# mLSTM values as one group of 512 columns in four PSUM banks, a value rank padded to 128 columns, and a bonus sum in another pair of banks

## The chip, the cores and the metric

The kernel runs on one core of a Trainium2 chip. The metric is the device time of that core in microseconds (us). The core has five engines that each run their own instructions in order: TensorE (PE, with its weight loads PEld), VectorE (DVE), ScalarE (ACT), GpSimd (POOL) and SyncE (SP), which issues most of the transfers.

## The reference

Two layers over 512 positions of 2048 features. Each layer normalises x, multiplies it by one wide matrix, cuts the product into the inputs of three branches, gates and joins their outputs, and multiplies by an output matrix:

```
for l in range(DEPTH):                       # 2 layers
    h = rms_norm(x, norm_g[l])               # 512 x 2048
    proj = h @ w_in[l]
    (ml_qk, ml_v, ml_i, ml_f, ml_o, ml_z, mla_cq, mla_ckv, mla_kr, mla_z,
     rw_mix, rw_z) = jnp.split(proj, offsets, axis=-1)     # ml_v: 512 columns
    y_ml  = mlstm_branch(...)                # 4 heads of 128
    y_mla = mla_branch(...)                  # 8 heads, softmax attention
    y_rw, v_first = rwkv7_branch(...)        # 8 heads of 64
    mixed = concat([silu(ml_z) * y_ml, silu(mla_z) * y_mla, silu(rw_z) * y_rw])
    x = x + mixed @ w_out[l]
return rms_norm(x, final_norm_g)

# in rwkv7_branch: in layer 1 the values are mixed with those of layer 0,
    v = v + (v_first - v) * jax.nn.sigmoid(v0 + (v @ v1) @ v2)     # v1: 512 x 32
# and the bonus is added to the output
    y = y + jnp.sum(r_h * k_h * r_k, axis=-1, keepdims=True) * v_h
```

Everything is float32. Sums over features run on TensorE.

## The kernel before

**Precision.** A float32 product is made of three passes over values split into a high and a low part: high times high, high times low, low times high (`passes`). ACT writes the high part of a weight block (L150), DVE or for some blocks POOL the low part (L151). Names follow: `raw_mv`, `whi_mv`, `wlo_mv` for the weights of the group mv; `xh`, `xl` for the normalised input, which lies feature-major in 16 blocks of 128 features.

**The projection as background work.** The wide matrix is cut into groups, named in `ORDER`: rk, rr, rv, rz for RWKV7, mq, mk, mv, mo, mz for the mLSTM, cq, ck, az for the attention, misc for narrow ones. A group has 256 columns of the matrix, as four weight blocks of 512 KB (`ws` streams them through two buffers in this order). `gemm` is a generator: for each block it issues 24 matmuls in two steps. All groups but mv give feature-major results: 512 positions are the moving columns, the weights are the stationary operand (L239). The mLSTM values must lie position-major, so for mv the input is stationary and the 256 weight columns move (`tmajor`, L235): 192 matmuls of 256 columns for each half of each 128-position block, two halves sharing a bank. The result goes through ACT (L597) to `mv_d` in DRAM.

**The foreground.** `rw_pair` runs four times a layer, for two RWKV7 heads each: a chain of small triangular solves by doublings. Its steps, in order, end in the PSUM tiles psw and psa (low-rank decays), psn (norm), psbo (bonus sum, `head_sum`, L714), psG, psTk, psTa, psTv (transposes), psQ, psR, psT, psX (doublings, L919), psW, psM, psN, psY. DVE and ACT work between two such steps, and background matmuls are to cover it: `bg.along` takes so many background steps for each step of the foreground. Then `rw_states` with `ml_head(0)` and `ml_head(1)`; then the attention's low-rank inputs with `ml_head(2)` and `ml_head(3)`; then `attention`.

**ml_head** makes scores (psSm), a weighted sum (psN), normalises it (`den`, `c`, `hn`, L1123 to L1141, with a square root on ACT), transposes it (psHT), gates it (`go`, L1151) and writes it to `mix_d` (L1152). Its SBUF pool is closed behind head 3, and the attention's pool `lp`, which holds the values `Vh` and `Vl`, takes its place: a write to `Vh` or `Vl` comes after the last reading of what lay there, the write of `go` to DRAM included.

**The attention** takes for each pair of heads the rotary part (psqr, then `rope` L1234 to L1237), queries and keys (psqn, pskn, L1263, split to qnh, qnl, knh, knl), values (psv, L1291, to Vh and Vl), scores (pssc), softmax (pp), transposes (pspt) and the weighted sum (pso).

**PSUM.** Eight banks: tag a (`bank`) two, tag b (`bank2`) two, tag g (`gbank`) three, tag h (`bank3`) one. Projection groups and psqr, psqn, pskn, psv take g; psbo, psSm, psHT take h; psG and ml_head's psN take b.

**Order.** Which instruction of an engine comes when is set at build time by a scheduler that simulates a timeline; on the chip each engine keeps that order.

Of the kernel before, what the change touches and what calls it, by code (L numbers as in the profile page):

```python
# [67 lines left out]
_REST = ["mq0", "mk0", "mv0", "mo0", "mz0", "rz1", "mq1", "mk1", "mv1", "mo1", "mz1", "cq0", "cq1", "ck0", "az0", "az1", "az2", "az3"]  # L68
# [5 lines left out]
def trunk(ctx, tc, a, out):  # L74
# [103 lines left out]
    def passes(hi, lo, xh, xl):  # L178
        return ((hi, xh), (hi, xl), (lo, xh))
# [38 lines left out]

    bg = Work()

    def gemm(l, name, finish, tmajor=False):

        def run():
            ps = [gbank(f"pg{u}_{name}{l}") for u in range(2)]
            xh, xl = xT[l]
            for kq in range(4):
                hi, lo = ws.get()
                for u in range(2):
                    for tb in range(2 * u, 2 * u + 2) if tmajor else (0,):
# [79 lines left out]
    def columns(l, name):  # L309
# [207 lines left out]
    for l in range(DEPTH):  # L517
# [72 lines left out]
        def park(kind, pr, l=l):  # L590

            def finish(u, ps):
                j = pr * 2 + u
                t = stage(f"{kind}{l}_{j}")
                if kind == "mv":
                    for b in range(2):
                        act(t[:, b * 256:b * 256 + 256], ps[:, b * 256:b * 256 + 256], AF.Copy,  # L597
                            scale=kept["rs"][:, 2 * u + b:2 * u + b + 1])
                    dma(mv_d[pr][:, u * 512:u * 512 + 512], t)
                    return  # L600
                if kind not in ("cq", "ck"):
                    ps = normed(stage(f"n{kind}{l}_{j}"), ps)
                if kind in ("mq", "mk"):
                    c = (0 if kind == "mq" else 4) + j
                    t, y = ps, t
                    act(y, ps, AF.Identity, scale=pc(R_CW + 24 + c), bias=pc(R_CB + c))
                    for d in range(1, 4):
                        stt(y[:, d:T], ps[:, 0:T - d], pc(R_CW + (3 - d) * 8 + c), y[:, d:T],
                            ALU.mult, ALU.add)
                    silu2(t, y, t)  # L610
                elif kind in SHIFT:
                    shift(t, ps, SHIFT[kind] + j)
                    if kind == "rv" and l > 0:
                        if j == 0:
                            kept["v1"] = bank(f"psv1_{l}")
                        mm(kept["v1"][0:32, :], lhsT=v1[:, j, :], rhs=t, start=(j == 0), stop=(j == 3))
                        if j == 3:
                            kept["vv"] = vv = rp.tile([128, T], F32R, name=f"vv{l}")
                            for r in (0, 64):
                                nc.scalar.copy(vv[r:r + 32], kept["v1"][0:32, :])  # L620
                                tt(vv[r + 32:r + 64], kept["v1"][0:32, :], vv[0:32].bitcast(F32), ALU.subtract)
                elif kind in ("az", "rz", "mz"):
                    silu2(t, ps, t)
                elif kind == "mo":
                    act(t, ps, AF.Tanh, scale=0.5)
                else:
                    normed(t, ps)
                dma(vf_d[j] if kind == "rv" and l == 0 else park_d[PARK[kind] + j], t)
            return finish

        for name in ORDER[l]:
            pr = int(name[2]) if name != "misc" else 0
            finish = misc_out if name == "misc" else park(name[0:2], pr)
            gemm(l, name, finish, tmajor=name[0:2] == "mv")
        if l == 0:
            x_tiles(0)
            for q in range(4):
# [43 lines left out]
            act(m[own], raw[own], AF.Copy)  # L681
            tt(m[other], raw[own], m[own].bitcast(F32), ALU.subtract)
        if l > 0:
            v1 = rp.tile([128, 4, 32], F32, name=f"v1_{l}")
            nc.gpsimd.dma_start(v1, a["rw_v1"][l - 1].rearrange("(k p) r -> p k r", p=128))
            raw = rp.tile([32, T], F32, tag="UV", name=f"v2r_{l}")
            nc.gpsimd.dma_start(raw, a["rw_v2"][l - 1])
            v2 = rp.tile([128, T], F32R, name=f"v2_{l}")
            for r in (0, 32):
                act(v2[r:r + 32], raw, AF.Copy)  # L690
                tt(v2[r + 64:r + 96], raw, v2[0:32].bitcast(F32), ALU.subtract)


        def rw_pair(p, l=l):
# [861 lines left out]
```

## Time and profile before

| | |
|---|---|
| median of 3 runs | 1966.4 us (1966.26 to 1967.19) |
| profiled execution | 1964.04 us, of which 1962.3 us from the first to the last instruction (the span) |
| granted TensorE clock, mean | 0.997 |
| busy share of the span | PE 98%, PEld 82%, DVE 63%, ACT 44%, POOL 7%, DMA engines 44% |
| matmuls of the projection with 256 columns (L235) | 768, 192 for each half group and layer |

A busy share is the time in which an engine had an instruction in work; PE's is nearly the whole span, since a matmul's record reaches from its start to the end of its drain and the next has started long before. So for TensorE the distance from start to start tells more than the durations. The rest of the span, some 30 us, is where PE has nothing in work.

### The profile page before, as it was taken

What the parts mean: (1) busy time and instruction counts of PE and PEld (TensorE: products, weight loads), DVE (VectorE), ACT (ScalarE), POOL (GpSimd) and SP (SyncE); (2) the same over time, 40 slices, a digit from 0 to 9 for tenths busy, and PEclk for the clock granted to TensorE, in tenths of its full rate; (3) what the DMA queues carried; (4) which work ended last, traced back from release to release, by engine and by line L of the source; (5) the groups of instructions that cost most, each with busy time, mean ns of one, the idle gap of its engine ahead of it and who ended that gap; (6) DMA issues with size and microseconds to landing.
All of it is one profiled execution on the core that took longest, in us unless ns stands there. A gap on an engine that the chain in (4) does not pass through costs nothing. (4 is left out here: it accounts for less than half of the span.)

```text
span 1962.3 us, 31796 instructions
## 1 busy us (share of the span) xinstructions
PE 1932.2 (98%) x12544; PEld 1607.1 (82%) x12544; DVE 1245.6 (63%) x2179; ACT 863.5 (44%) x1509; POOL 136.4 (7%) x168
## 2 busy tenths in 40 slices
PE   8999999999999999999999999999999999999998
PEld 6888888888888878788888788988878888788886
DVE  6876776685766398533366558676847676884343
ACT  6534352434556356422263234433434564563233
POOL 4010010100000031000001001010100000210000
PEclk9999999999999999999999999999999999999999
DMA  5443444335655443334444444344345564343334
GB/s 178 131 141 106 126 127 119 115 110 173 188 167 177 120 119 121 103 136 133 135 111 138 121 122 129 118 131 122 106 125 189 167 209 137 105 133 115 118 121 158
DMA packets 246394, 264.86 MB, mean 135 GB/s; under 512 B 49972, under 2 KB 178174, under 8 KB 246246
## 3 DMA queue, kind: packets, MB, share of 16 engines
q1 hardware_dynamic: 245398, 261.88, 43.8%
q8 instruction: 98, 1.61, 0.3%
q0 software_dynamic: 848, 0.97, 0.2%
q14 instruction: 50, 0.41, 0.1%
HBM read 212.45 MB, written 50.35 MB: 134 GB/s over the span
## 5 line engine op out<-in xcount | busy, mean ns | idle before, releaser
L1405 PE MATMUL po<-whi_o,mh 128*128 128x512 f32 x512 | 200.2, 391 | 0.1
L1405 PE MATMUL po<-whi_o,ml 128*128 128x512 f32 x512 | 199.3, 389 | 0.0
L151 DVE TENSOR_TENSOR wlo_o<-raw_o,whi_o 128x1024 fp32r<-128x1024 f32 x64 | 78.3, 1225 | 188.7 <-ACT whi_o L150 187.6
L1405 PE MATMUL po<-wlo_o,mh 128*128 128x512 f32 x512 | 187.8, 390 | 0.0
L150 ACT ACTIVATE whi_o<-raw_o 128x1024 fp32r<-128x1024 f32 x64 | 67.7, 1059 | 204.7 <-PE po L1405 168.2
L1405 PEld LDWEIGHTS po<-whi_o,mh 128*128 128x128 f32 x512 | 96.1, 188 | 20.1 <-DVE Vl L254 0.6
L1405 PEld LDWEIGHTS po<-wlo_o,mh 128*128 128x128 f32 x512 | 96.0, 188 | 20.0
L1405 PEld LDWEIGHTS po<-whi_o,ml 128*128 128x128 f32 x512 | 96.2, 188 | 19.7
L239 PE MATMUL pg_az<-xl,whi_az 128*128 128x512 f32 x256 | 100.7, 393 | 0.0
L239 PE MATMUL pg_az<-xh,whi_az 128*128 128x512 f32 x256 | 100.6, 393 | 0.0
L239 PE MATMUL pg_az<-xh,wlo_az 128*128 128x512 f32 x256 | 99.5, 394 | 0.0
L235 PE MATMUL pg_mv<-whi_mv,xh 128*128 128x256 f32 x256 | 72.9, 285 | 0.0
L235 PE MATMUL pg_mv<-whi_mv,xl 128*128 128x256 f32 x256 | 72.7, 285 | 0.0
L235 PE MATMUL pg_mv<-wlo_mv,xh 128*128 128x256 f32 x256 | 72.4, 285 | 0.0
L770 POOL TENSOR_TENSOR bk<-kk,Ei 64x512 f32<-64x512 f32 x16 | 26.5, 1657 | 505.2 <-DVE kk L757 176.5
L151 DVE TENSOR_TENSOR wlo_az<-raw_az,whi_az 128x1024 fp32r<-128x1024 f32 x32 | 39.1, 1223 | 31.0 <-ACT whi_az L150 30.8
L239 PEld LDWEIGHTS pg_az<-xh,wlo_az 128*128 128x128 f32 x256 | 48.1, 188 | 9.5
L239 PEld LDWEIGHTS pg_az<-xh,whi_az 128*128 128x128 f32 x256 | 48.1, 188 | 9.4
L239 PEld LDWEIGHTS pg_az<-xl,whi_az 128*128 128x128 f32 x256 | 48.2, 188 | 9.3
L239 PE MATMUL pg_rk<-xh,whi_rk 128*128 128x512 f32 x128 | 50.9, 401 | 1.3 <-ACT xh L252 1.3
L239 PE MATMUL pg_rk<-xl,whi_rk 128*128 128x512 f32 x128 | 51.5, 403 | 0.0
L150 ACT ACTIVATE whi_az<-raw_az 128x1024 fp32r<-128x1024 f32 x32 | 33.7, 1053 | 39.7 <-PE pg_az L239 26.6
(576 smaller groups left out, 5547.7 us busy)
## 6 DMA issues: line engine op xcount, KB each, us to landing
raw_o<-in_w_out_dram SPq DMA_DIRECT2D x64, 512.0 KB
raw_az<-in_w_in_dram SPq DMA_DIRECT2D x32, 512.0 KB
raw_rk<-in_w_in_dram SPq DMA_DIRECT2D x16, 512.0 KB
raw_rr<-in_w_in_dram SPq DMA_DIRECT2D x16, 512.0 KB
raw_rv<-in_w_in_dram SPq DMA_DIRECT2D x16, 512.0 KB
raw_rz<-in_w_in_dram SPq DMA_DIRECT2D x16, 512.0 KB
raw_mq<-in_w_in_dram SPq DMA_DIRECT2D x16, 512.0 KB
raw_mk<-in_w_in_dram SPq DMA_DIRECT2D x16, 512.0 KB
```

What stands on the lines that cost most here:

```text
L150: act(hi, raw, AF.Copy)
L151: (nc.gpsimd if name[0] == "u" or name in ("misc0_0", "misc0_1") else nc.vector).tensor_tensor(lo, raw, hi.bitcast(F32), ALU.subtract)
L235: mm(ps[u][:, (tb % 2) * 256:(tb % 2) * 256 + 256], lhsT=xx[:, sl], rhs=w[:, i, :], start=(k == 0 and n == 0 and tb % 2 == 0), stop=(k == ...
L239: mm(ps[u], lhsT=w[:, i, u * 128:(u + 1) * 128], rhs=xx, start=(k == 0 and n == 0), stop=(k == 15 and n == 2))
L770: nc.gpsimd.tensor_tensor(bk[q, :, slot, :], x[q].rearrange(c64, t=64), Ei[q].rearrange(c64, t=64), ALU.mult)
L1405: mm(pss[tb], lhsT=xx[:, sl], rhs=w, start=(k == korder[0] and j == 0), stop=(k == korder[15] and j == 2))
```

## The change

Three things. The mLSTM values become one group, `mv`, of all 512 columns, in the place of mv0; mv1 leaves the order, so that mo1 follows mk1. The generator `gemm_rows` issues it: eight weight blocks of 256 rows by 512 columns (the same 512 KB), for each block four banks (three of tag g and the one of tag h) of six matmuls of 512 columns, and a step behind every second bank: 16 steps, as many as mv0 and mv1 had together. That makes 192 matmuls of 512 columns a layer in place of 384 of 256. Four ACT copies of 512 columns and eight transfers of 256 columns replace eight copies of 256 columns and four transfers of 512. Second, `v1` is padded with zeros from 32 to 128 columns, and the matmul of L616 writes 128 rows. Third, psbo takes its bank from tag b, since tag h is now held by the group mv.

```diff
-_REST = ["mq0", "mk0", "mv0", "mo0", "mz0", "rz1", "mq1", "mk1", "mv1", "mo1", "mz1", "cq0", ...
+_REST = ["mq0", "mk0", "mv", "mo0", "mz0", "rz1", "mq1", "mk1", "mo1", "mz1", "cq0", ...
...
-    def gemm(l, name, finish, tmajor=False):
+    def gemm(l, name, finish):
...
-                    for tb in range(2 * u, 2 * u + 2) if tmajor else (0,):
-                        sl = slice(tb * 128, (tb + 1) * 128)
-                                if tmajor:
-                                    mm(ps[u][:, (tb % 2) * 256:(tb % 2) * 256 + 256], lhsT=xx[:, sl],
-                                       rhs=w[:, i, :], start=(k == 0 and n == 0 and tb % 2 == 0),
-                                       stop=(k == 15 and n == 2), skip_group_check=True)
...
+    def gemm_rows(l, name, finish):
+
+        def run():
+            ps = [(gbank, bank3, gbank, gbank)[tb](f"pg{tb}_{name}{l}") for tb in range(4)]
+            xh, xl = xT[l]
+            for kh in range(8):
+                hi, lo = ws.get()
+                for tb in range(4):
+                    sl = slice(tb * 128, (tb + 1) * 128)
+                    for i in range(2):
+                        k = kh * 2 + i
+                        for n, (w, xx) in enumerate(passes(hi, lo, xh[k], xl[k])):
+                            mm(ps[tb], lhsT=xx[:, sl], rhs=w[:, i, :], start=(k == 0 and n == 0),
+                               stop=(k == 15 and n == 2))
+                    if kh == 7:
+                        finish(tb, ps[tb])
+                        if tb == 3:
+                            bg.done.add(name)
+                    if tb % 2:
+                        yield
         bg.todo.append(run())
...
+            if name == "mv":
+                for kh in range(8):
+                    ws.add(mv_columns(l, kh), (2, 512), f"mv{l}_{kh}")
+                continue
...
-                if kind == "mv":
-                    for b in range(2):
-                        act(t[:, b * 256:b * 256 + 256], ps[:, b * 256:b * 256 + 256], AF.Copy,
-                            scale=kept["rs"][:, 2 * u + b:2 * u + b + 1])
-                    dma(mv_d[pr][:, u * 512:u * 512 + 512], t)
-                    return
...
-                        mm(kept["v1"][0:32, :], lhsT=v1[:, j, :], rhs=t, start=(j == 0), stop=(j == 3))
+                        mm(kept["v1"], lhsT=v1[:, j, :], rhs=t, start=(j == 0), stop=(j == 3))
...
+        def values_out(tb, ps, l=l):
+            t = stage(f"mv{l}_{tb}")
+            act(t, ps, AF.Copy, scale=kept["rs"][:, tb:tb + 1])
+            for pr in range(2):
+                dma(mv_d[pr][:, tb * 256:tb * 256 + 256], t[:, pr * 256:pr * 256 + 256])
...
-            v1 = rp.tile([128, 4, 32], F32, name=f"v1_{l}")
+            v1 = rp.tile([128, 4, 128], F32, name=f"v1_{l}")
+            nc.vector.memset(v1[:, :, 32:128], 0.0)
...
-            ps = head_sum(bo, "AR", "psbo", bank3)
+            ps = head_sum(bo, "AR", "psbo", bank2)
```

The change also moves other instructions, since the scheduler is run anew. Three places. A number behind a name tells the layer's head, pair or block apart; the last one is the tile's.

On PE in layer 0, pair 3, between the steps psR and psT of the first doubling, before (18 projection matmuls stand between the two, of which the first two and the last are shown; psT is eight instructions, of which two are shown):

```order
L825 MATMUL psR_3_3435<-UV_3_3332,GG_3_3150 64x64 x2
L235 MATMUL pg_mv_5063<-wlo_mv_0_4995,xh_0_132 128x256
L235 MATMUL pg_mv_5063<-whi_mv_0_4994,xh_1_133 128x256
...
L235 MATMUL pg_mv_5064<-whi_mv_0_4994,xl_2_150 128x256
L919 MATMUL psT_3_3493<-Qa_3_3398,X_3_3303 32x32 x4
L919 MATMUL psT_3_3492<-Qa_3_3398,X_3_3303 32x32 x4
```

The steps of the pair and the projection take turns there. In the changed kernel at the same place:

```order
L851 MATMUL psR_3_3413<-UV_3_3332,GG_3_3150 64x64 x2
L232 MATMUL pg_mk_4810<-xl_3_151,whi_mk_0_4734 128x512
L232 MATMUL pg_mk_4810<-xh_3_135,wlo_mk_0_4735 128x512
...
L232 MATMUL pg_mk_4811<-xh_1_133,wlo_mk_0_4735 128x512
L945 MATMUL psT_3_3459<-Qa_3_3376,X_3_3303 32x32 x4
L945 MATMUL psT_3_3458<-Qa_3_3376,X_3_3303 32x32 x4
```

Pair 3 of layer 0 now lies beside mk0, of which eight matmuls of 512 columns stand between the two steps; the group mv lies beside pair 2 in layer 0 and beside pairs 1 and 2 in layer 1.

On PE at the end of layer 1's head 3, where the attention begins, before (twelve psqn of the attention's first head and twelve psqr come only behind these rows):

```order
L239 MATMUL pg_az_15974<-xh_12_8412,wlo_az_3_16039 128x512
L239 MATMUL pg_az_15974<-xh_13_8413,whi_az_3_16038 128x512
L239 MATMUL pg_az_15974<-xl_13_8429,whi_az_3_16038 128x512
L1145 MATMUL psHT_3_15555<-idf,hn_3_15550 128x128
L239 MATMUL pg_az_15974<-xh_13_8413,wlo_az_3_16039 128x512
L1145 MATMUL psHT_3_15555<-idf,hn_3_15550 128x128 x3
L239 MATMUL pg_az_15974<-xh_14_8414,whi_az_3_16038 128x512
...
L239 MATMUL pg_az_15974<-xl_15_8431,whi_az_3_16038 128x512
L239 MATMUL pg_az_15974<-xh_15_8415,wlo_az_3_16039 128x512
L1263 MATMUL psqr_0_16116<-cqh_0_15182,whi_uqr_0_16069 128x512
```

There the transpose psHT stands among matmuls of az, and az outlasts it. In the changed kernel (the last chunk of psN, six pskn of head 1, twelve psqn of head 2, the transpose psHT, six pskn of head 2):

```order
L1140 MATMUL psN_3_1_15066<-mvh_3_15059,mel_3_15142 128x130
L1289 MATMUL pskn_1_15858<-ckh_0_14807,whi_uqk_1_15798 128x512
...
L1289 MATMUL pskn_1_15858<-ckh_1_14808,wlo_uqk_1_15799 128x512
L1289 MATMUL psqn_2_15978<-cqh_0_14799,whi_uqk_2_15837 128x512
...
L1289 MATMUL psqn_2_15978<-cqh_3_14802,wlo_uqk_2_15838 128x512
L1171 MATMUL psHT_3_15172<-idf,hn_3_15167 128x128 x4
L1289 MATMUL pskn_2_15995<-ckh_0_14807,whi_uqk_2_15837 128x512
...
L1289 MATMUL pskn_2_15995<-ckh_1_14808,wlo_uqk_2_15838 128x512
L1352 MATMUL pssc_0_2_15903<-knh_0_15791,qnh_0_15780 128x384
```

The projection az now ends before head 3 is done, and head 3's last steps stand among the attention's first ones: psv of the first pair, psqn and pskn of two heads come ahead of psHT.

On DVE at the same place, before:

```order
L1132 TENSOR_TENSOR c_3_15533<-c_3_15533,var_3_15532 128x4
L270 RECIPROCAL c_3_15533<-c_3_15533 128x4
L1134 SCALAR_TENSOR_TENSOR c_3_15533<-c_3_15533,den_3_15531 128x4
L1141 TENSOR_SCALAR hn_3_15550<-psN_3_0_15448,c_3_15533 128x128
L1141 TENSOR_SCALAR hn_3_15550<-psN_3_1_15449,c_3_15533 128x128
L1150 SCALAR_TENSOR_TENSOR go_3_15560<-go_3_15560,gz_3_15561 128x512
L542 TENSOR_TENSOR sg_naz_6_16086<-pg_az_15973,rb_9678 128x512
L254 TENSOR_TENSOR ml_12_17496<-mr_12_17493,mh_12_17495 128x512
L1151 SCALAR_TENSOR_TENSOR go_3_15560<-psHT_3_15555,prm_291,go_3_15560 128x512
```

There `hn` follows the normalisation at once. In the changed kernel:

```order
L1158 TENSOR_TENSOR c_3_15150<-c_3_15150,var_3_15149 128x4
L285 RECIPROCAL c_3_15150<-c_3_15150 128x4
L1160 SCALAR_TENSOR_TENSOR c_3_15150<-c_3_15150,den_3_15148 128x4
L269 TENSOR_TENSOR knl_1_15866<-pskn_1_15858,knh_1_15865 128x512
L1167 TENSOR_SCALAR hn_3_15167<-psN_3_0_15065,c_3_15150 128x128
L1167 TENSOR_SCALAR hn_3_15167<-psN_3_1_15066,c_3_15150 128x128
L1176 SCALAR_TENSOR_TENSOR go_3_15177<-go_3_15177,gz_3_15178 128x512
L1177 SCALAR_TENSOR_TENSOR go_3_15177<-psHT_3_15172,prm_291,go_3_15177 128x512
L269 TENSOR_TENSOR Vl_0_15803<-psv_0_0_15804,Vh_0_15802 128x512
L269 TENSOR_TENSOR Vl_0_15803<-psv_0_1_15819,Vh_0_15802 128x512
```

A split of the attention's keys (knl) now stands inside the normalisation of head 3, and the first Vl behind `go`.

## Rows read from the trace of the kernel before

**Rows 1.** The page's busy times: engine, busy us (share of the span), instructions.

```profile
PE 1932.2 (98%) x12544; PEld 1607.1 (82%) x12544; DVE 1245.6 (63%) x2179; ACT 863.5 (44%) x1509; POOL 136.4 (7%) x168
```

**Rows 2.** What PE waited for, whole span: us in total, times, longest.

```profile
PE psv L1291 <- DVE qrf L1236: 5.0, 2, 2.6
...
PE psT L919 <- DVE Qa L931: 1.1, 1, 1.1
...
PE psqn L1263 <- POOL wlo_uqk L151: 0.7, 1, 0.7
PE psTk L808 <- DVE GG L801: 0.6, 1, 0.6
PE psTv L779 <- DVE TX L862: 0.6, 1, 0.6
PE psbo L714 <- DVE psbox L254: 0.4, 1, 0.4
PE psQ L919 <- DVE T L881: 0.3, 1, 0.3
```

**Rows 3.** The page's costliest groups, PE with 256 columns: busy us, mean ns.

```profile
L235 PE MATMUL pg_mv<-whi_mv,xh 128*128 128x256 f32 x256 | 72.9, 285 | 0.0
```

**Rows 4.** Timeline of PE in the group mv: start us, us, instruction.

```profile
272.73 0.28 PE L235 MATMUL pg_mv<-whi_mv,xh 128*128 128x256 f32 x1
...
273.93 0.28 PE L235 MATMUL pg_mv<-whi_mv,xl 128*128 128x256 f32 x1
```

**Rows 5.** Timeline of PE in the group misc, 512 columns.

```profile
1000.05 0.39 PE L239 MATMUL pg_misc<-xh,whi_misc 128*128 128x512 f32 x1
...
1002.77 0.39 PE L239 MATMUL pg_misc<-xh,whi_misc 128*128 128x512 f32 x1
```

**Rows 6.** Timeline of PE at a matmul with v1 (psv<-sg_rv,v), layer 1.

```profile
1086.87 0.39 PE L239 MATMUL pg_rv<-xh,whi_rv 128*128 128x512 f32 x1
1087.19 1.04 PE L616 MATMUL psv<-sg_rv,v 128*32 128x512 f32 x2
1088.16 0.50 PE L239 MATMUL pg_rv<-xl,whi_rv 128*128 128x512 f32 x1
```

**Rows 7.** Timeline of PE, full-width float32 matmuls of 128 columns.

```profile
605.41 1.05 PE L1199 MATMUL psrb<-idf,rw 128*128 128x128 f32 x8
606.22 0.48 PE L239 MATMUL pg_az<-xl,whi_az 128*128 128x512 f32 x1
```

**Rows 8.** Timeline of PE around psT, layer 0, pair 3.

```profile
426.92 0.28 PE L235 MATMUL pg_mv<-whi_mv,xl 128*128 128x256 f32 x1
428.27 0.92 PE L919 MATMUL psT<-Qa,X 32*32 32x32 f32 x64 [1.08 <-DVE Qa L931]
429.12 0.38 PE L235 MATMUL pg_mv<-wlo_mv,xh 128*128 128x256 f32 x1
```

**Rows 9.** Timeline of DVE at the end of layer 1's head 3.

```profile
1653.29 0.16 DVE L1123 SCALAR_TENSOR_TENSOR den<-psN,gcol 128x2 f32<-128x2 f32 x1 [0.47 <-PE psN L1114]
...
1661.23 0.74 DVE L1151 SCALAR_TENSOR_TENSOR go<-psHT,prm,go 128x512 f32<-128x512 f32 x1
```

**Rows 10.** Timeline of ACT at the same place.

```profile
1654.38 1.28 ACT L269 ACT_TABLE_LOAD   x1
1655.68 0.30 ACT L269 ACTIVATE c<-c,epst 128x4 f32<-128x4 f32 x1
...
1657.33 0.62 ACT L150 ACTIVATE whi_uqr<-raw_uqr 128x512 fp32r<-128x512 f32 x1
```

**Rows 11.** Timeline of SP's queue in layer 0: a write to DRAM, its reading.

```profile
731.69 0.34 SPq L1376 DMA_DIRECT2D mix_d<-ao  x1
733.69 0.34 SPq L1396 DMA_DIRECT2D mr<-mix_d  x1
```

**Rows 12.** The tile Vh: duration ns min/median/max, first and last start.

```profile
L252 ACT ACTIVATE Vh<-psv x16: 575/595/598, 700.0 to 1771.7; 128x512 fp32r<-128x512 f32 x16
```

**Rows 13.** The tile Vl, the same columns.

```profile
L254 DVE TENSOR_TENSOR Vl<-psv,Vh x16: 671/679/681, 701.7 to 1772.9; 128x512 fp32r<-128x512 f32 x16
```

More of the change, by code (lines that the diff above doesn't have):

```diff
@@ L67 @@
 SHIFT = {"rr": 0, "rk": 4, "rv": 8}
-_REST = ["mq0", "mk0", "mv0", "mo0", "mz0", "rz1", "mq1", "mk1", "mv1", "mo1", "mz1", "cq0", "cq1", "ck0", "az0", "az1", "az2", "az3"]
+_REST = ["mq0", "mk0", "mv", "mo0", "mz0", "rz1", "mq1", "mk1", "mo1", "mz1", "cq0", "cq1", "ck0", "az0", "az1", "az2", "az3"]
 ORDER = [["rk0", "misc", "rr0", "rv0", "rz0", "rk1", "rr1", "rv1"] + _REST,
@@ L228, in run @@
                 for u in range(2):
-                    for tb in range(2 * u, 2 * u + 2) if tmajor else (0,):
-                        sl = slice(tb * 128, (tb + 1) * 128)
-                        for i in range(4):
-                            k = kq * 4 + i
-                            for n, (w, xx) in enumerate(passes(hi, lo, xh[k], xl[k])):
-                                if tmajor:
-                                    mm(ps[u][:, (tb % 2) * 256:(tb % 2) * 256 + 256], lhsT=xx[:, sl],
-                                       rhs=w[:, i, :], start=(k == 0 and n == 0 and tb % 2 == 0),
-                                       stop=(k == 15 and n == 2), skip_group_check=True)
-                                else:
-                                    mm(ps[u], lhsT=w[:, i, u * 128:(u + 1) * 128], rhs=xx,
-                                       start=(k == 0 and n == 0), stop=(k == 15 and n == 2))
+                    for i in range(4):
+                        k = kq * 4 + i
+                        for n, (w, xx) in enumerate(passes(hi, lo, xh[k], xl[k])):
+                            mm(ps[u], lhsT=w[:, i, u * 128:(u + 1) * 128], rhs=xx,
+                               start=(k == 0 and n == 0), stop=(k == 15 and n == 2))
                     if kq == 3:
@@ L245, in run @@
                     yield
+        bg.todo.append(run())
+    def gemm_rows(l, name, finish):
[8 more added lines that the diff above has]
+                        k = kh * 2 + i
+                        for n, (w, xx) in enumerate(passes(hi, lo, xh[k], xl[k])):
+                            mm(ps[tb], lhsT=xx[:, sl], rhs=w[:, i, :], start=(k == 0 and n == 0),
[6 more added lines that the diff above has]
+                        yield
         bg.todo.append(run())
@@ L324, in columns, with mv_columns, src @@
         return misc if name == "misc" else block
+    def mv_columns(l, kh):
+        def src(v):
+            dma(v, a["w_in"][l, kh * 256:(kh + 1) * 256, C_V:C_V + 512].rearrange("(a p) f -> p a f", p=128))
+        return src
     def out_rows(l, nb_, ks):
@@ L629, in park @@
             return finish
+        def values_out(tb, ps, l=l):
[3 more added lines that the diff above has]
+                dma(mv_d[pr][:, tb * 256:tb * 256 + 256], t[:, pr * 256:pr * 256 + 256])
         for name in ORDER[l]:
-            pr = int(name[2]) if name != "misc" else 0
-            finish = misc_out if name == "misc" else park(name[0:2], pr)
-            gemm(l, name, finish, tmajor=name[0:2] == "mv")
+            if name == "mv":
+                gemm_rows(l, name, values_out)
+                continue
+            gemm(l, name, misc_out if name == "misc" else park(name[0:2], int(name[2])))
         if l == 0:
@@ L683, in trunk @@
         if l > 0:
-            v1 = rp.tile([128, 4, 32], F32, name=f"v1_{l}")
-            nc.gpsimd.dma_start(v1, a["rw_v1"][l - 1].rearrange("(k p) r -> p k r", p=128))
+            v1 = rp.tile([128, 4, 128], F32, name=f"v1_{l}")
+            nc.vector.memset(v1[:, :, 32:128], 0.0)
+            nc.gpsimd.dma_start(v1[:, :, 0:32], a["rw_v1"][l - 1].rearrange("(k p) r -> p k r", p=128))
             raw = rp.tile([32, T], F32, tag="UV", name=f"v2r_{l}")
```

## The prediction

> **What bounds the kernel now.** I read the page's busy times first: PE is busy for 1932.2 of 1962.3 us, 98%, DVE for 63%, ACT for 44% [rows 1]. So the time is PE's stream plus its waits, and an edit counts only if it shortens what PE issues or changes what PE waits for. A matmul's duration doesn't tell its cost, since neighbours overlap: those with 256 columns last 285 ns [rows 3], but begin every 120 ns (ten steps in 273.93 − 272.73 = 1.20 us) [rows 4]. Those with 512 columns begin every 0.2267 us (twelve steps in 2.72 us) [rows 5]. Next the waits of PE: those that carry a name from a pair's chain or from the attention's start are 5.0, 1.1, 0.7, 0.6, 0.6, 0.4 and 0.3 us [rows 2]. They are small, but so is everything here.
>
> All sums below are changes of the span, 1962.3 us, with 1.7 us around it in the profiled execution (1964.04). The median of the runs is 2.4 us above that one, so I add the sum to the median. About 0.2% (3.9 us) is what a measurement of this kernel can tell from no change.
>
> **A: half as many matmuls, twice as wide.** Before, three groups of 256 matmuls [rows 3], 768 × 0.120 = 92.2 us [rows 4]. After, 384 × 0.2267 = 87.1 us [rows 5]. That is −5.1. Two columns' worth of work is the same; what goes is a part per matmul, 2 × 0.120 − 0.2267 = 0.013 us. The new ones change bank every six matmuls instead of every twelve. The misc rows span no bank change that I could see a price for; ten ns each over 64 changes would be 0.6, so the bounds are −4.5 and −5.1.
>
> The Trainium skill (TensorE: Matmul & The Clock Gate, "Wait — 56ns, not 53.3ns?") gives warm back-to-back matmuls as columns over 2.4 GHz plus 2.5 ns, 215.7 ns at 512 columns. By it 768 narrow ones would be 83.9 and 384 wide ones 82.8, and this term −1.0 instead of −5.1. This trace disagrees, with 120 and 226.7 ns.
>
> **B: v1 padded.** A narrow matmul with v1 takes 1088.16 − 1086.87 − 0.227 = 1.06 us of PE's time for 512 columns in two instructions, and its form is 128×32, while its neighbours' is 128×128 [rows 6]. The nearest full-width float32 product is psrb: eight instructions of 128 columns take 0.81 us from their start to the next projection's [rows 7]. Two instructions of 512 columns hold as many columns, so 0.81 to 0.9 each, and four such matmuls give −0.6 to −1.0. If the form costs nothing, 0. I take −0.7. The memset (two more rows on DVE, which is idle for 37%) comes long before the value projection, and only the rank's 32 rows are read.
>
> **C: waits beside mv.** Layer 0's psT waits for DVE [rows 8]. The matmul ahead of it starts at 426.92, so the next could at 427.04; psT starts at 428.27, 1.23 late, where the row of waits has 1.08, a factor of 1.14. The order shows why: 18 narrow matmuls are 18 × 0.120 = 2.2 us of cover for what DVE and ACT do between the two steps. In the other pairs, 8 wide ones and more stand between steps. The waits of psT, psTk, psTv, psbo and psQ sum to 3.0 us [rows 2], all of one pair in each layer that ran beside narrow matmuls, so 3.4 with the factor. In the changed order psT has eight others beside it (8 × 0.2267 = 1.8), which is no more than 2.2; but psQ was itself late there, and DVE starts its part as soon as psQ is done, beside the full chain of the other pairs, which shows no such wait. I take −3.3, with −1.5 as the other bound if half of it moves along.
>
> psbo from tag b costs at most what it is kept waiting for a bank: psG needs both banks of that tag, and the second half of psG now waits for ACT's copy of psbo. The order puts 4 to 18 projection matmuls there, 0.9 to 4 us, against a copy of 0.6 (the same kind as in [rows 12]). With a thin place in head 2's scores I take +0.3 for new waits, 0 to 1.5. The copies of mv to DRAM (ACT, SP) run behind PE and cost nothing as long as mo0's banks, which they free, are wanted 18 matmuls later; without that cover, one copy, 0.6.
>
> **D: where layer 1 goes over to attention.** The order moves az ahead of the end of head 3, so that nothing of the projection is left to cover it.
>
> - *First stall, at psqn of head 2.* It needs the bank of pskn of head 1, which knl frees on DVE, and knl stands behind `c` of head 3. From den's start to the end of the square root are 1653.29 to 1655.98, 2.69 us [rows 9, 10], then two more DVE steps and knl. On ACT one weight split of 0.62 now stands ahead of the table load [rows 10], and knh behind the root, 0.6 like Vh [rows 12]; knl is 0.68 like Vl [rows 13]. With 0.3 for hand-overs: 2.69 + 0.62 + 0.6 + 0.68 + 0.3 = 4.9. PE has six pskn to do meanwhile, 6 × 0.2267 = 1.36. Stall 3.5.
> - *Second stall, at pskn of head 2.* Its bank is that of the first psv, freed by the first Vl. Vh and Vl lie where head 3's `go` lay, so ACT and DVE must first see `go` written to DRAM. PE has just issued psHT, and nothing stands between. `go` 0.74 [rows 9], the write 2.00 from its issue to that of the transfer that waited for it [rows 11], Vh 0.60, Vl 0.68 [rows 12, 13], hand-overs 0.3: 4.3.
> - Between them, steps of head 3 and the attention alternate with two or three matmuls of cover. I count three waits of the size of those in [rows 2] (0.3 to 0.4), 1.0.
> - What goes: psqn's wait for POOL, 0.7, and psv's for the rope, two of 5.0 in all, the longest 2.6; layer 1's is the other, 2.4 [rows 2]. With the factor, −3.5.
>
> Together 3.5 + 4.3 + 1.0 − 3.5 = +5.3, bounds +2.5 and +7.5: below, if the write lands when the reader's issue is still to come; above, if the pieces don't overlap and the rope's wait stays.
>
> The table load is in [rows 10] 1.28 us, and the root starts 0.02 behind it. The Trainium skill (ScalarE: Activation LUTs, "What ACT_TABLE_LOAD costs") has 1283 ns and 1380 ns of drain for a switch. By it the first stall would be 1.4 longer and the sum as much higher; the row shows no drain behind the load.
>
> **The sum.** −5.1 − 0.7 − 3.3 + 0.3 + 5.3 = −3.5 us, 1962.9. With all bounds one way, −5.1 − 1.0 − 3.4 + 0 + 2.5 = −7.0, with all the other way, −4.5 − 0 − 1.5 + 1.5 + 7.5 = +3.0. So this case by itself: 1959.4 to 1969.4.
>
> **Rivals.**
>
> 1. *The hand-over costs no more than it did.* D is zero, if the two stalls are taken out of later ones (PE is behind DVE and ACT in the attention's first steps anyway, so that time lost there is saved at psv and pssc). For it: the old start had its 3.1 us of waits at just this place [rows 2]. Against it: PE is 98% busy. −5.1 − 0.7 − 3.3 + 0.3 = −8.8, 1957.6.
> 2. *Slower than before: DVE and ACT behind the wait for `go`.* Both engines stand still until the write has landed, some 3 us, and behind Vl on DVE and Vh on ACT are the softmax of the first scores, a table load and the splits of head 2. If the pspt that follow wait for that, a third stall of 4 to 8 us comes on top: Vh twice, the load, an exponential, the reciprocals, 1.2 + 1.28 + 0.6 + 0.5 = 3.6 for the first block alone [rows 10, 12], against some 3.4 us of scores and pskn on PE. Against it: that cover nearly suffices. It decides from 7.4 us of further stall; I put it at +4, 1970.4.
> 3. *The waits beside mv don't go, they move* to the pairs that now run beside it. C is zero: −3.5 + 3.3, 1966.2.
> 4. *Wide matmuls save little.* A is −1.0: 1967.0. It is a mechanism of this kernel only if a bank change every sixth matmul costs some 60 ns; no row shows one. The skill's rule named under A would give the same.
>
> **How the numbers follow.** The forecast 0.50, rival 1 0.23, rival 2 0.12, rival 3 0.09, rival 4 0.06. Of the forecast's 0.50 I put 0.20 below 1962.5, the bound of faster, and 0.30 within. Faster: 0.23 + 0.20 = 0.43. Same: 0.30 + 0.09 + 0.06 = 0.45. Slower: 0.12. For 8 in 10 I leave out rival 2 and the lower edge of rival 1: 1956.8 to 1969.0; the forecast's own bounds lie within it but for 0.4.
>
> **What would show it.** Matmuls of mv at starts 0.227 us apart and 384 of them (A). Four v1 matmuls of 128×128 with less than 0.3 us of idle ahead (B). No wait of psT, psTk, psTv and psQ above 0.3 (C). In the list of PE's waits, psqn for DVE's knl with about 3.5 and pskn for Vl with about 4.3, each once (D). I am wrong if these two are under 1 us, if a wait for a PTl, pp or Vl of several us stands behind them, or if PE's waits rise in layer 0, whose attention starts as before.

## The result and the profile after

The changed kernel takes 1990.03 us (median of 4 runs, 1989.72 to 1992.03) against 1966.8 (4 runs, 1966.26 to 1967.94). The ratio is 1.0123 with an interval of 1.0111 to 1.0135: 23 us slower. The prediction was 1962.9 in 1956.8 to 1969.0. The profiled execution took 1990.15 us with a span of 1988.5, 26.2 longer than before. Its page begins so (busy us, share of the span, instructions, against [rows 1]; then the granted TensorE clock of the 40 slices in tenths):

```profile
span 1988.5 us, 31032 instructions
...
PE 1941.1 (98%) x12160; PEld 1591.6 (80%) x12160; DVE 1246.6 (63%) x2180; ACT 866.7 (44%) x1505; POOL 135.6 (7%) x168
...
PEclk9999999999999999999999999999999999899999
```

PE is no less busy in share, and one slice, the 35th (1690 to 1740 us), no longer has a 9 in the clock. The waits of PE, in total us, times, longest, against [rows 2]:

```profile
PE pskn L1289 <- DVE Vl L269: 4.4, 1, 4.4
PE psqn L1289 <- DVE knl L269: 4.0, 2, 3.4
PE psSm L1126 <- DVE me L1133: 4.0, 4, 1.8
PE psT L945 <- DVE Qa L957: 3.6, 3, 1.9
...
PE psv L1317 <- DVE qrf L1262: 2.6, 1, 2.6
...
PE psqn L1289 <- ACT whi_uqk L150: 1.9, 1, 1.9
PE psTk L834 <- DVE GG L827: 1.8, 1, 1.8
PE psv L1317 <- ACT qnh L267: 1.7, 1, 1.7
```

All waits of this view sum to 38.2 us, before to 21.0: +17.2. The two stalls that the prediction worked out for the hand-over are there, 4.4 and 3.4 us (psqn's other wait for knl, 0.6, is in layer 0). What is new beside them stands in three places: psqn for whi_uqk, psv for qnh and the longest of psSm's waits for me, 1.8, belong to the same hand-over, ahead of the two; psSm's other three, 2.1 together, stand in layer 0's heads (`me` is what DVE makes of a head's scores, and psSm has one bank); psT and psTk belong to the pairs' solves, where the prediction had said that waits would go. PE at the hand-over (start, duration, instruction, in brackets the idle time ahead and its releaser):

```profile
1695.04 0.39 PE L1289 MATMUL pskn<-ckh,wlo_uqk 128*128 128x512 f32 x1
1698.79 0.50 PE L1289 MATMUL psqn<-cqh,whi_uqk 128*128 128x512 f32 x1 [3.36 <-DVE knl L269]
...
1700.39 0.63 PE L1289 MATMUL psqn<-cqh,whi_uqk 128*128 128x512 f32 x1
1700.82 0.63 PE L1289 MATMUL psqn<-cql,whi_uqk 128*128 128x512 f32 x1
...
1702.95 0.90 PE L1171 MATMUL psHT<-idf,hn 128*128 128x128 f32 x4
1708.22 0.76 PE L1289 MATMUL pskn<-ckh,whi_uqk 128*128 128x512 f32 x1 [4.37 <-DVE Vl L269]
```

DVE, SP's queue and ACT there:

```profile
1703.89 0.75 DVE L1177 SCALAR_TENSOR_TENSOR go<-psHT,prm,go 128x512 f32<-128x512 f32 x1 [4.04 <-PE psHT L1171]
1707.39 1.29 DVE L269 TENSOR_TENSOR Vl<-psv,Vh 128x512 fp32r<-128x512 f32 x2 [2.75 <-ACT Vh L267]
```

```profile
1704.67 0.34 SPq L1178 DMA_DIRECT2D mix_d<-go  x1
1706.67 0.34 SPq L1422 DMA_DIRECT2D mr<-mix_d  x1
```

```profile
1706.76 1.08 ACT L267 ACTIVATE Vh<-psv 128x512 fp32r<-128x512 f32 x2 [7.10 <-DMA mix_d<-go]
```

The chain of the second stall reads down these rows: psHT at 1702.95, `go` at 1703.89, the write to DRAM issued at 1704.67 and its follower at 1706.67 (2.00 us, as in [rows 11]), Vh at 1706.76 after ACT had stood idle for 7.10 us, Vl at 1707.39, pskn at 1708.22.

The rows of PE hold one thing more: psqn's matmuls of 512 columns start 0.43 us apart (1700.39, 1700.82), not 0.227 [rows 5]. The granted clock in stretches of 8 us (stretch, length, busy us and instructions of PE, PEld, DVE, ACT, POOL, PEclk, DMA share, GB/s):

```profile
1664.00:1672.00 8.00, 6.09 (x34) 5.02 (x34) 6.29 (x11) 6.07 (x11) 0.12 (x1) 1.00 0.29 88
1672.00:1680.00 8.00, 7.36 (x30) 5.61 (x30) 7.92 (x10) 3.88 (x9) 3.25 (x2) 0.79 0.87 251
1680.00:1688.00 8.00, 4.81 (x30) 4.50 (x31) 7.86 (x14) 4.82 (x13) 2.04 (x1) 0.91 0.19 46
1688.00:1696.00 8.00, 7.39 (x37) 5.93 (x36) 3.98 (x14) 3.10 (x10) 1.82 (x2) 0.88 0.24 67
1696.00:1704.00 8.00, 5.06 (x16) 3.81 (x16) 2.26 (x7) 2.62 (x5) 1.25 (x1) 0.79 0.28 82
1704.00:1712.00 8.00, 3.78 (x10) 3.12 (x10) 3.31 (x8) 4.61 (x9) 0.51 (x1) 0.69 0.21 66
1712.00:1720.00 8.00, 8.00 (x46) 6.73 (x45) 5.68 (x14) 3.89 (x9) 2.19 (x2) 0.89 0.41 117
```

The clock is below full speed in six of the seven stretches, 8 × (0.21 + 0.09 + 0.12 + 0.21 + 0.31 + 0.11) = 8.4 us short of full (in part of it PE had nothing to do). The kernel before goes over between 1664 and 1696, at 1.00 all through, with a psv wait in it:

```profile
1664.00:1672.00 8.00, 5.54 (x24) 3.92 (x22) 7.92 (x9) 5.09 (x9) 5.00 (x3) 1.00 0.75 240
1672.00:1680.00 8.00, 7.24 (x45) 6.51 (x46) 7.91 (x11) 4.71 (x8) 2.72 (x2) 1.00 0.48 134
```

**Why the projection was out.** The last matmul of az starts at 1664.96, but head 3 ends only with `go` at 1703.89; before, at 1662.05 and 1661.23 [rows 9]. The lateness is older than head 3. The pairs of RWKV7 in layer 1, from psw's first matmul to psY's last, last longer. Pair 3, psw's first and psY's group, first in the changed kernel:

```profile
1376.44 0.40 PE L745 MATMUL psw<-whh,w 128*128 128x512 f32 x1
```

```profile
1484.17 1.10 PE L860 MATMUL psY<-UV,GG 128*64 128x64 f32 x32
```

and in the kernel before:

```profile
1367.10 0.40 PE L719 MATMUL psw<-whh,w 128*128 128x512 f32 x1
```

```profile
1462.49 1.10 PE L834 MATMUL psY<-UV,GG 128*64 128x64 f32 x32
```

From the first to the end of the group (1484.17 + 1.10, 1462.49 + 1.10) that is 108.8 us, and was 96.5; pairs 1 and 2 last 99.2 and 96.8, and lasted 94.0 and 94.3. PE issues projection in the extra time, and this projection is then missing later: counted at 0.227 us for 512 columns and 0.120 for 256, the projection matmuls that start within pairs 1 to 3 are 84.8, 78.9 and 91.1 us, and were 79.9, 80.0 and 79.5, so 15.4 more in all. The wide group stands beside pairs 1 and 2, not beside pair 3.

Layer 0 loses something too. Layer 1's first pair (psw's first row) starts at 1020.82, before at 1017.74: 3.1 later, though the wide group saves half of A, 2.5, ahead of it.

**A and B.** The group mv, twelve steps:

```profile
279.63 0.39 PE L253 MATMUL pg_mv<-whi_mv,xh 128*128 128x512 f32 x1
...
282.35 0.39 PE L253 MATMUL pg_mv<-whi_mv,xh 128*128 128x512 f32 x1
```

2.72 us, 0.227 each as in [rows 5], and 384 of them, against 768 at 0.120. The matmul with v1 in layer 1:

```profile
1089.86 0.39 PE L232 MATMUL pg_rv<-xl,whi_rv 128*128 128x512 f32 x1
1090.09 1.02 PE L634 MATMUL psv<-sg_rv,v 128*128 128x512 f32 x2
1090.55 0.79 PE L232 MATMUL pg_rv<-xh,wlo_rv 128*128 128x512 f32 x1
1091.18 0.40 PE L232 MATMUL pg_rv<-xh,whi_rv 128*128 128x512 f32 x1
```

and the row that follows those of [rows 6] in the kernel before:

```profile
1088.50 0.39 PE L239 MATMUL pg_rv<-xh,wlo_rv 128*128 128x512 f32 x1
```

From the projection matmul ahead to the second one behind are 1.32 us; before, from 1086.87 to 1088.50, 1.63. That is 0.31 less for each of four, 1.2.

### The profile page after: what moved, and what is told of

It reads as the page before. It is cut to its first block, busy times and chain, and to the rows that moved or that the text cites. A ratio compares the mean times of both kernels' runs of the same rounds, so it can differ in the third digit from the quotient of the medians.

```text
span 1988.5 us, 31032 instructions
## 1 busy us (share of the span) xinstructions
PE 1941.1 (98%) x12160; PEld 1591.6 (80%) x12160; DVE 1246.6 (63%) x2180; ACT 866.7 (44%) x1505; POOL 135.6 (7%) x168
## 4 chain that ended last, share of the span: by engine, by line
PE 82%; DVE 7%; DMA 4%; ACT 3%; issue 3%; SPq 0%; ACTq 0%; DVEq 0%
PE po L1431 18%; PE pg_mv L253 4%; PE pg_mo L232 4%; PE pg_cq L232 4%; PE pg_rk L232 4%; PE pg_mz L232 4%; PE pg_rr L232 4%; PE pg_az L232 4%; PE pg_rv L232 4%; PE pg_mk L232 3%; PE pg_mq L232 3%; PE pg_rz L232 3%; PE pssc L1352 2%; PE pg_misc L232 2%; PE psqn L1289 2%
## 5 line engine op out<-in xcount | busy, mean ns | idle before, releaser
L1431 PEld LDWEIGHTS po<-whi_o,mh 128*128 128x128 f32 x512 | 96.2, 188 | 20.4 <-DVE Vl L269 0.6
L232 PE MATMUL pg_az<-xh,wlo_az 128*128 128x512 f32 x256 | 99.2, 395 | 0.1
L232 PE MATMUL pg_rz<-xl,whi_rz 128*128 128x512 f32 x128 | 50.9, 398 | 0.0
L232 PE MATMUL pg_rv<-xh,wlo_rv 128*128 128x512 f32 x128 | 50.4, 401 | 0.4 <-DVE wlo_rv L151 0.4
L232 PE MATMUL pg_mk<-xl,whi_mk 128*128 128x512 f32 x128 | 50.7, 396 | 0.0
L232 PE MATMUL pg_rk<-xh,wlo_rk 128*128 128x512 f32 x128 | 50.7, 400 | 0.0
```

The costliest lines, as they stand in the source:

```text
L232: mm(ps[u], lhsT=w[:, i, u * 128:(u + 1) * 128], rhs=xx, start=(k == 0 and n == 0), stop=(k == 15 and n == 2))
L1431: mm(pss[tb], lhsT=xx[:, sl], rhs=w, start=(k == korder[0] and j == 0), stop=(k == korder[15] and j == 2))
```

## The experiments

Fourteen kernels, in four groups (e1 to e4, e5 to e8, e9 to e11, e12 to e14) of which each shared a chip and the runs of the kernel before; its medians there are 1964.64, 1965.43, 1965.39 and 1966.47 us. The ratio behind a time is against these runs, with its interval, and kernels of different groups are compared by it. The theory after the first look (theory A in the texts, not the prediction's term A): the loss is the hand-over, since the projection is used up beside the longer pairs of layer 1 (A1: because of where mv now stands; A2: because of its wide matmuls).

### 1. Does cover bring the time back? `e1_fill96`

The changed kernel with the first block's matmuls of az0 to az3 in layer 1 issued twice; the first pass is thrown away by the second's start.

```diff
-                    for i in range(4):
+                    for again in ((1, 0) if kq == 0 and l == 1 and name in FILL else (0,)):
+                        for i in range(4):
...
```

> The changed kernel with 96 more projection matmuls in layer 1: the first weight block of az0 to az3 is multiplied twice, the first product being overwritten. 96 x 0.227 = 21.8 us more for PE; the order shows az outlasting head 3 again, by 26 rows. Theory A (the loss is the missing cover at layer 1's hand-over: waits of psqn, psv, psSm and pskn of 13.2 us there against 3.1 before, and a granted clock of 0.5 to 0.8 behind them): those waits and the low clock go, some 10 + 8 us, so 1990 + 21.8 - 18 = 1994, between 1989 and 1998. Theory B (the loss is in how the group mv runs, its four banks, or in the pairs): nothing goes, 2010 to 2012.

Measured: 1993.55 us (1989.59 to 1996.31, 4 runs), ratio 1.0145 [1.013, 1.016]. 96 matmuls × 0.227 = 21.8 us of useless work cost 3.5 us by the medians, and 5.7 if each is set against the kernel before on its own chip, so 16 to 18 of them lie in time that PE had lost. The stalls at pskn for Vl and at psqn for knl are gone from its waits, which begin again with psv's for the rope, as in [rows 2]:

```profile
PE psv L1319 <- DVE qrf L1264: 5.0, 2, 2.6
```

In its profile az again ends behind `go` (last starts 1692.67 and 1687.16). That is what the theory says: most of the loss is missing cover at the hand-over.

### 2. The parts one by one: `e2_narrow_together`, `e3_psbo_bank`, `e4_v1_padded`

Each is the kernel before with one edit: mv1 directly behind mv0 in the order; psbo in tag b; v1 padded.

```diff
-_REST = ["mq0", "mk0", "mv0", "mo0", "mz0", "rz1", "mq1", "mk1", "mv1", "mo1", ...
+_REST = ["mq0", "mk0", "mv0", "mv1", "mo0", "mz0", "rz1", "mq1", "mk1", "mo1", ...
```

```diff
-            ps = head_sum(bo, "AR", "psbo", bank3)
+            ps = head_sum(bo, "AR", "psbo", bank2)
```

```diff
-                        mm(kept["v1"][0:32, :], lhsT=v1[:, j, :], rhs=t, start=(j == 0), stop=(j == 3))
+                        mm(kept["v1"], lhsT=v1[:, j, :], rhs=t, start=(j == 0), stop=(j == 3))
...
+            v1 = rp.tile([128, 4, 128], F32, name=f"v1_{l}")
+            nc.vector.memset(v1[:, :, 32:128], 0.0)
...
```

> The kernel before with mv1 moved directly behind mv0; all matmuls of mv stay narrow, no other edit. Theory A1 (what lengthened the chain of layer 1's pair 3 is the place of mv: its finishing costs DVE nothing, and pair 3 now has mq1, mk1 and mo1 beside it): psG to psQ of pair 3 takes some 40 us as in the changed kernel, not 34, and the time is 1975 to 1992. Theory A2 (the wide matmuls themselves change what the scheduler puts between the steps): 1964 to 1970; the order here leaves az outlasting head 3 by six rows as before.

Measured: 1960.41 (1959.08 to 1962.46, 9 runs), 0.9979 [0.9969, 0.9989]. The place alone makes the kernel faster. A1 fell; the time lies below A2's range as well, so neither had a gain from the place.

> The kernel before with psbo in a bank of tag b alone. Both theories: within 2 us of 1966.4. If the waits of psG for the copy of psbo were a part of the loss, 1969 or more.

Measured: 1965.67, 1.0005 [0.9996, 1.0014].

> The kernel before with v1 padded to 128 columns alone. -0.7 us as in the prediction, 1965.7; 1966.4 if the form of the matmul costs nothing. The idle time of 0.1 us ahead of each such matmul goes.

Measured: 1964.28, 0.9997 [0.9987, 1.0006]. Neither of these two can be told from no change in the order of before.

### 3. Width alone: `e5_split_halves`, `e6_split_layer1`, `e11_split_layer0`

The changed kernel with each matmul of mv as two of 256 columns into the same bank: place, banks and steps stay. In e6 so in layer 1 only, in e11 in layer 0 only.

```diff
-                            mm(ps[tb], lhsT=xx[:, sl], rhs=w[:, i, :], start=(k == 0 and n == 0),
+                            for c in (0, 256):
+                                mm(ps[tb][:, c:c + 256], lhsT=xx[:, sl], rhs=w[:, i, c:c + 256],
...
```

> The changed kernel with each matmul of 512 columns of the group mv issued as two of 256, into the two halves of the same bank; groups, blocks, four banks, copies, v1 and psbo stay as changed. 768 matmuls of 0.120 again, +5.1 us by that alone. Theory A2 (narrow matmuls make the scheduler put less projection time between the steps of the pairs beside them, wide ones more, and that excess comes back as missing cover at the hand-over): the order leaves az outlasting head 3 by six rows, the waits of psqn for knl and pskn for Vl go, and the time is near that of the narrow mv0 and mv1 side by side, 1958 to 1966. Theory B (banks, blocks, copies or the place of mv): 1990 + 5 = 1995.

Measured: 1973.03 (1967.46 to 1975.83, 6 runs), 1.0037 [1.0024, 1.0051]. 17 of the 23 us are gone (1.0123 to 1.0037), though PE has some 5 us more to issue. It is still above the 1958 to 1966 that A2 gave.

> The same, but only layer 1's mv is split, layer 0's stays at 512 columns. Theory A2: layer 0 keeps its cover (az outlasts head 3 there by some 146 rows in any case), layer 1 gets its own back: 2.5 us less than with both layers split, or up to 2 more if layer 0's pairs wait more beside wide matmuls; 1956 to 1966. If the loss were spread over both layers: 1975 to 1985.

Measured: 1968.53 (1963.13 to 1972.29, 10 runs), 1.0013 [1.0002, 1.0023], 2.5 us above the range.

> The changed kernel with mv split into halves in layer 0 alone, layer 1 wide: the other half of the run with layer 1 split (1968.5). If the loss is layer 1's: the changed kernel's 1990 plus 2.5 for the narrow matmuls, 1988 to 1995, with the waits of psqn for knl (3.4) and pskn for Vl (4.4) as in the changed kernel. If layer 0 had a share in it: 1975 to 1985.

Measured: 1987.31 (1986.65 to 1994.2, 4 runs), 1.0123 [1.0103, 1.0143], the ratio of the changed kernel (the time is 0.7 below the range). Its waits begin as those of the changed kernel do:

```profile
PE pskn L1292 <- DVE Vl L272: 4.4, 1, 4.4
PE psqn L1292 <- DVE knl L272: 3.4, 1, 3.4
```

The three together show that the trigger is the width of mv's matmuls in layer 1. In e5 and e6 the pairs of layer 1 last 92.4, 92.5, 96.2 and 91.9, 92.5, 97.9 us (pairs 1 to 3), in e11 99.7, 94.2, 110.3, in the changed kernel 99.2, 96.8, 108.8. The projection within the three pairs, counted as above, is 236.7 us in e5 and e6 (in e2 too), and 254.8 in e11 as in the changed kernel: 18.1 less with narrow matmuls in layer 1.

### 4. Another order with the wide group: `e7_wide_other_order` and its control `e8_narrow_other_order`

Layer 1's order in e7, made from the changed kernel, and in e8, made from the kernel before. Both also gain lines that hold the heads back until mk0 (in e7 mv too) is done, and the attention's inputs until mz1 is (`bg.ensure`):

```diff
+_R1 = ['rz1', 'mo0', 'mz0', 'mo1', 'mz1', 'mv', 'mq0', 'mk0', 'mq1', 'mk1', 'cq0', ...
+_R1 = ['rz1', 'mo0', 'mz0', 'mo1', 'mz1', 'mv0', 'mv1', 'mq0', 'mk0', 'mq1', 'mk1', ...
```

> The changed kernel, mv wide in both layers, with another order of the groups in layer 1 alone: rz1, mo0, mz0, mo1, mz1, mv, then mq0, mk0, mq1, mk1. The order leaves az outlasting head 3 by 32 rows. If the missing cover is the cause, the hand-over's waits go and the narrower stream shows: 1958 to 1964. If wide matmuls cost by themselves, 1980 or more.

Measured: 1977.59 (1971.84 to 1984.38, 5 runs), 1.0063 [1.0043, 1.0082].

> The kernel before with the same other order in layer 1 (mv0 and mv1 side by side in the place of mv), v1 and psbo as before. Control of the run ahead: the difference of the two is what the three edits bring where cover is not missing: the sum of terms A and B, 5.8 us, so 1964 to 1970.

Measured: 1973.8 (1973.4 to 1976.9, 4 runs), 1.0048 [1.0033, 1.0063]. Both miss. The order, with the lines that go with it, costs some 8 us even with narrow matmuls (its waits for Qa alone are 6.0 us). Wide ones come out 3.8 above narrow ones, where I had expected them 5.8 below; the two intervals overlap, so that "above" is not shown. The part on the hand-over did come: in e7 az ends behind `go` (last starts 1678.24 and 1671.39), and no wait for knl or Vl is in its list.

```profile
PE psT L920 <- DVE Qa L932: 6.0, 3, 3.0
```

### 5. Width in layer 0, and psbo's bank in the good order: `e9_wide_layer0_only`, `e10_together_psbo_b`, `e13_together_v1`

All three start from e2. e9 has the wide group, and psbo in tag b with it, in layer 0 only (first new line); e10 has psbo in tag b in both layers (second); e13 has v1 padded as in e4.

```diff
-            ps = head_sum(bo, "AR", "psbo", bank3)
+            ps = head_sum(bo, "AR", "psbo", (bank2, bank3)[l])
+            ps = head_sum(bo, "AR", "psbo", bank2)
```

> The narrow mv0 and mv1 side by side (second run), but layer 0's as the wide group in four banks, with psbo in tag b in that layer alone; layer 1 has mv0 and mv1 in two banks of tag g each, psbo in tag h, v1 unpadded. If wide matmuls pay where az outlasts head 3 anyway: 1960.4 - 2.5 + 0.5 = 1958.4. If four banks or the longer pairs cost in layer 0, as the third of a per cent by which the run with layer 1 split stayed above the kernel before suggests: 1962 to 1968.

Measured: 1966.73 (1962.8 to 1974.13, 10 runs), 1.0012 [1.0001, 1.0024]. That is the second of the two ranges, and 0.0033 or 6.5 us above e2: in layer 0 the wide group with psbo in tag b costs more than A gives there. The two came together here.

> The narrow mv0 and mv1 side by side with psbo in tag b, no other edit. The run with the split halves, 1973, differs from this one by four banks, blocks of 256 rows, fewer and longer copies, and v1. If psbo's bank is what separates 1973 from 1960.4: 1968 or more. If it costs what it cost alone: 1960.4 + 1.0 = 1961.4.

Measured: 1970.62 (1966.44 to 1976.72, 10 runs), 1.0029 [1.0018, 1.004]. Against e2 that is 10 us for one bank; the same edit on the order of before cost 1.0. In its profile (span 1966.4 us, e2's 1959.1) layer 1's first psw starts at 1022.30 us, in e2's at 1014.28, so that the difference of these two executions stands in layer 0. A part are waits in layer 0's heads that e2 does not have:

```profile
PE psSm L1100 <- DVE me L1107: 2.9, 3, 1.2
```

In e5, with psbo in tag b too, layer 1 starts at 1022.92.

> The narrow mv0 and mv1 side by side (1960.4) with v1 padded: -0.4 as v1 alone gave on the kernel before, 1960.0; the version that should beat both kernels. Above 1962 if the layout of memory or order that the larger v1 brings costs.

Measured: 1960.36 (1959.45 to 1961.23, 8 runs), 0.997 [0.996, 0.9981]. With e2 this beats both kernels; the padding adds nothing to e2 that could be told.

### 6. Is one wait the cause? `e12_values_own_memory` and its control `e14_before_own_memory`

Vh and Vl take their memory from a small pool of their own, shared with the heads' queries and keys, so that they no longer wait for the pool of `go`; e14 is the same edit in the kernel before.

```diff
-            Vh = lp.tile([128, 4, 256], F32R, tag="Vh", name=f"Vh{l}_{hp}")
+            Vh = qp.tile([128, 4, 256], F32R, tag="Q0", name=f"Vh{l}_{hp}")
...
```

> The changed kernel with the attention's Vh and Vl taken from a pool that they share with the heads' queries and keys alone, which are last read by head 3's scores; the pool that holds go is still taken over by the rest of the attention. The wait of Vh and Vl for go's write to DRAM is gone, and in the order Vl and knl now stand ahead of head 3's hn and go. az still ends before head 3 does. Theory (the second stall is the wait for that pool): the wait of pskn for Vl, 4.4, and most of psqn for knl, 3.4, go, and the low clock behind them, some 5: 1974 to 1981. If the missing cover only moves the waits on to the next steps: 1985 or more.

Measured: 1990.11 (1985.75 to 1992.26, 4 runs), 1.012 [1.0105, 1.0135]: nothing gained. The wait of 4.4 us is gone, and PE waits for the next things instead, at half the clock (last windows):

```profile
1707.55 0.36 PE L1320 MATMUL psv<-whi_uv,ckh 128*128 128x256 f32 x1 [3.94 <-DVE qrf L1265]
...
1712.02 0.69 PE L1355 MATMUL pssc<-knh,qnh 128*128 128x384 f32 x1 [1.93 <-ACT pp L1360]
```

```profile
1704.00:1712.00 8.00, 2.54 (x12) 2.28 (x12) 4.61 (x7) 1.86 (x4) 1.75 (x1) 0.75 0.69 199
1712.00:1720.00 8.00, 7.98 (x35) 6.73 (x36) 5.84 (x17) 4.82 (x12) 0.00 (x0) 0.61 0.03 9
```

> Control: the kernel before with the same change of memory for Vh and Vl. There az outlasts head 3, so nothing waits for go: within 3 us of the kernel before, 1963 to 1969.

Measured: 1966.67, 1.0003 [0.9994, 1.0013]. So with e1: the missing cover is the cause; which wait it shows up at is not.

## Why the prediction was wrong

**What bounds the kernel** held: PE's stream and its waits. What I left out is the clock, which fell to half behind some of the waits.

**A** held: −5.1 by the intervals. **B** had the right sign and was too small: 1.2 by the starts, for 0.7 (0 to 1.0), since [rows 6] stops at the first matmul behind and the second was late as well. In the whole time e4 and e13 could not tell it from nothing.

**C was wrong in its sign, and it is the first step that failed.** It expected the waits beside mv to go, −3.3. psTv, psbo and psQ are indeed gone from the list, but psT and psTk now sum to 5.4 us, against 3.0 for all five before [rows 2]: +2.4. psT waits three times, once for 1.9 us, and with wide matmuls for cover:

```profile
1342.33 0.39 PE L232 MATMUL pg_rz<-xh,wlo_rz 128*128 128x512 f32 x1
1344.66 0.98 PE L945 MATMUL psT<-Qa,X 32*32 32x32 f32 x64 [1.94 <-DVE Qa L957]
...
1346.16 0.63 PE L232 MATMUL pg_rz<-xl,whi_rz 128*128 128x512 f32 x1
1346.59 0.63 PE L232 MATMUL pg_rz<-xh,wlo_rz 128*128 128x512 f32 x1
```

Here eight wide matmuls stand between psR and psT, as in the row of the order that I had quoted (there, at 429.72, psT waits for 1.26, before 1.08); DVE needs longer than they last. Its rows show why:

```profile
1342.07 1.22 DVE L151 TENSOR_TENSOR wlo_rz<-raw_rz,whi_rz 128x1024 fp32r<-128x1024 f32 x1
1343.20 0.68 DVE L281 SCALAR_TENSOR_TENSOR sg_mz<-sg_mz,sg_nmz 128x512 f32<-128x512 f32 x1
1343.92 0.59 DVE L957 TENSOR_TENSOR Qa<-psQ,mq 64x128 f32<-64x128 f32 x2
```

psQ began at 1339.80 and psR followed at 1339.99, but Qa comes on DVE only behind the finishing of the group mz and a weight split, nearly four us later. So the argument that "DVE starts its part as soon as psQ is done" failed: what stands ahead on DVE counts, not only the matmuls on PE. And the wait of 1.94 is followed by matmuls 0.43 us apart.

**psbo's bank**, a term of +0.3 with a bound of 1.5, failed too. In the order nearest to the changed one it costs 10 us (e10). How much of that is in the changed kernel was not tried apart; its layer 0 loses 5.6 (3.1 and the 2.5 saved), with psSm's three waits there.

**D was right in what it described and too small in what it counted.** The order of events, az out before head 3, was forecast; the first stall was 3.4 for 3.5, the second 4.4 for 4.3, with the chain as worked out. The rope's wait of layer 1 went, as said. Not counted were three waits of the same place, whi_uqk 1.9, qnh 1.7 and me 1.8, for which the prediction had 1.0; 13.2 us of waits stand there in all, and 8.4 us of lowered clock beside them, in part within the waits. The upper bound of 7.5 was the step that made the range too narrow: it priced the waits that I could name, though the order showed that nothing of the projection was left there to cover PE at any of its steps.

**The sum** of the span's +26.2 us: −5.1 (A), −1.2 (B), +17.2 (waits), and about +6 for the clock (0.994 × 1988.5 against 0.997 × 1962.3, that is 11.9 − 5.9 us short, ±2 by the rounding). The remaining 9 are found only by difference. An estimate from the two traces, each distance from start to start on PE against the median of its form, puts some 4 of them directly beside waits (starting again) and some 5 beside none, most of these in layer 0. By place the same estimate gives +5.6 up to 1000 us (layer 0), +5.2 from there to 1595 us (layer 1's pairs) and +22.6 behind, against −7.1 of work saved. So by it the hand-over cost some 22 us where D had 5.3 and at most 7.5.

**The rivals.** Rival 1 needed that time lost at the hand-over be saved later; the runs show none saved. Rival 2 had the right side, but its mechanism, a third stall at pspt, is not in the list: pspt waits 1.1 us as before. Rival 3 came true in part and worse than it said, since the waits grew. Rival 4 fell with A.

**What caused it**, as far as the runs show: wide matmuls in layer 1 (e5, e6, e11) go with longer pairs; the longer pairs use up the projection; the attention then begins without cover; 16 to 18 of the 23 us are in that place (e1). That the pairs take more projection is counted (254.8 us against 236.7 with narrow matmuls in layer 1); why the scheduler, which counts background steps, puts more of it between the steps of pair 3 when mv is wide was only argued, not tested apart. Of the 11 and 7 us by which e5 and e6 stay above e2, by the ratios, psbo's bank can be the larger part (10 us in that order by e10, and e5 and e10 start layer 1 at the same time to 0.6 us); the changed kernel with psbo back in tag h was not tried. Open is why the order of e7 and e8 went the other way.

## What to carry to other kernels

Work that runs as background is a stock: an edit that makes a phase use more of it is paid where the stock runs out, so before costing an edit look up in the order when the last background instruction comes and what stands behind it uncovered, and price that whole stretch, not the waits that you can name. To test such a reason, add useless background work: if the time hardly rises, cover was what was missing, while taking away one of its waits only shows the next one. And try the edit's parts alone: here the place of the group was worth −4 us, its width in one layer most of +23, and a bank that cost 1 us in one order cost 10 in another.

## What the hardware showed that I had not expected

After some waits of PE the granted clock was at half, 1.2 GHz by the spacing of 0.43 in place of 0.227 us, for several us: behind the psT wait of 1.94 (rows above), behind the stalls of 3.36 and 4.37, and once for some 14 us in e1 at a wait of only 0.72 for psSm, ahead of which PE had run short matmuls of 130 columns (psN). In e1's four stretches of 4 us from 592 on it is 0.77, 0.50, 0.50 and 0.53; the second:

```profile
596.00:600.00 4.00, 4.00 (x15) 3.42 (x14) 2.42 (x9) 1.78 (x7) 0.00 (x0) 0.50 0.43 131
```

It is not the length of the wait alone. Layer 0's psv waits for the rope for 2.58 us in both kernels, before at 697.64, changed at 700.73: in the stretch from 696 to 704 the clock is 0.79 before and 1.00 in the changed kernel. And the wait of 2.40 in layer 1's hand-over of the kernel before has 1.00 (the windows at 1664 and 1672 above). With it goes a scatter: e10's ten runs lie between 1966.44 and 1976.72, the two slowest (1975.73 and 1976.72) at a mean clock of 0.994 and the others at 0.995 to 0.999, where the kernel before on that chip stays within 3.2 us. What decides whether a wait costs the clock stays open.
